# Hybrid attention and convolution layer: last six attention units spaced wider, second attention norm moved three steps back

## The chip, the cores and the metric

One core of one Trainium2 chip runs one program. The metric is the device time in microseconds (us) of an execution. Engines by the profile's names: PE is TensorE's matmul, PEld its weight load, DVE VectorE, ACT ScalarE, POOL GpSimd, SP SyncE. SBUF is the on-chip memory, PSUM the memory that PE writes. L642 is line 642 of the kernel.

## The reference, cut to what matters

```python
h = rms_norm(x, norm_mix_g)                    # x: (1, 1024, 1024) float32
q, k, v, u, gate = jnp.split(h @ w_in, splits, axis=-1)
q, k = rms_norm(q per head), rms_norm(k per head)
a = sliding_window_gqa(q, k, v, sinks, rel_bias)   # window 128, 8 heads of 64, 2 kv heads
c = conformer_conv(u, gate, ...)               # 512 channels
mix = jnp.concatenate([rms_norm(a, attn_out_g), rms_norm(c, conv_out_g)], axis=-1)
x = x + mix @ w_out
x = x + jnp.square(jax.nn.relu(rms_norm(x, norm_mlp_g) @ w_mlp_up)) @ w_mlp_down
```

Only the attention `a`, its norm, and where both stand among the matmuls of `mix @ w_out` are touched.

## The kernel before

All activations lie with features on the 128 partitions and tokens along the free side; the 1024 tokens are two halves h = 0 and 1 of 512. A dense product is made with each operand split in two parts (`whi`, `wlo` of the weight, the first and second slice of `mix` or `x1g` of the activation) and three matmuls of 128x128 by 128x512 for each block.

**Dense steps.** `build` (L212) runs a chain of generators, `dense`, one step at a time. Steps 0 to 47 are the input projections. Steps 48 to 55 are `out_conv(0)` and 56 to 63 `out_conv(1)` (L711): the half of the output projection that reads the convolution's `mix`, one step for each of 8 row blocks, 12 matmuls a step, and DVE adds the product to x (L720). Steps 64 to 71 are `out(0)` and 72 to 79 `out(1)` (L723): the other half, that reads the attention's `mix`, 12 matmuls a step, DVE adds again (L731). From step 80 `up_first` begins the MLP. Each step also has ACT and DVE split the weights of the next one (L162, L163).

**Side work.** Ahead of each dense step the words of `SIDE[k]` (L40) are issued. An attention unit is one of 4 head pairs j and one of 4 pairs of query blocks bp, named by the digits "j bp", and has three words:
- `A` (`attn_a` L551 and `attn_b` L576): score matmuls into two `sc` banks (`sc<-kh,Q`), four ACT copies to an SBUF tile `s` (L571), bias and maximum on DVE (L572), four Exp on ACT (L586), scaling on DVE (L592).
- `T` (`attn_t`): eight transposes of `s` into two `tr` banks (`tr<-ident,s`, L89) and two DVE copies to a tile `pT` (L596).
- `V` (`attn_v`): the products with v into the one `o` bank (`o<-pT,v`) and an ACT copy over the unit's slice of `Q` (L596).

The twelve late units, in the order of `U_LATE` (10, 11, 20, 21, 30, 31, 12, 13, 22, 23, 32, 33), have their `A` at the steps of `LATE`, `T` three steps and `V` five steps later. Units with bp 0 and 1 make half 0, bp 2 and 3 half 1.

**Norms.** `N0` and `N1` (`norm_attn`, `norm_half` L623) norm the attention of half 0 and 1 over four head pairs, each by three words: squares on ACT and sums on DVE (`nacc`, L628 to L632); a sum over partitions on PE into the `o` bank (`o<-ones,nacc`), DVE (L206) and a power on POOL (L207); a broadcast on PE into an `sc` bank (`sc<-ident,rc`), then for each of the four pairs a scaling on DVE (L642), an ACT cast (L652) and a DVE subtraction (L653), which make that half's `mix`. `out(0)` can't begin before N0's `mix`, `out(1)` not before N1's.

**Buffers and order.** PSUM has two banks each of `mm` (dense products), `sc` and `tr`, one of `o` and one of `x`. The tiles `s` and `pT` share eight SBUF buffers of tag `t`. The order on each engine is fixed when the program is built: from the program's order, from what is pinned, and from when inputs and buffers come free; so an instruction may stand on its engine before or behind the step that issued it. Units and norms issue no DMA.

Of the kernel before, what the change touches and what calls it, by code (L numbers as in the profile page):

```python
# [35 lines left out]
EVAC = {11: 'vaa', 2: 'aaa', 0: 'aaa', 9: 'vav', 10: 'avv', 8: 'vaa', 6: 'vav', 12: 'aaa', 4: 'aaa', 14: 'aav', 13: 'vaa', 3: 'aav', 15: 'aav', 1: 'aaa', 7: 'aaa', 5: 'aaa'}  # L36
ORDER = "u0,u1,u2,u3,v,q1,q2,q3"
U_EARLY, U_LATE = (9, 13, 17, 21), ("10", "11", "20", "21", "30", "31", "12", "13", "22", "23", "32", "33")
LATE = (43, 44, 47, 48, 51, 51, 52, 53, 54, 55, 56, 57)
SIDE = {2: "rs", 3: "st4 st0", 5: "rb st0", 6: "st4", 7: "st4", 12: "c0", 20: "c1", 28: "c2",  # L40
# [5 lines left out]
for n, at in enumerate(U_EARLY):  # L46
    SIDE[at] = SIDE.get(at, "") + f" A0{n}"
    SIDE[at + 4] = SIDE.get(at + 4, "") + f" T0{n}"
    SIDE[39 + n] = SIDE.get(39 + n, "") + f" V0{n}"
for u, at in zip(U_LATE, LATE):  # L50
    SIDE[at] = SIDE.get(at, "") + " A" + u
# [1099 lines left out]
```

## Time and profile before

| What | us |
|---|---|
| Median of 3 runs | 995.53 (990.51 to 996.84) |
| The profiled execution | 990.88 |
| Its span, first to last instruction | 989.1 |

The span is 1.78 us shorter than the profiled execution. PE's share is time in which a matmul is under way; matmuls overlap, so a busy PE can still be waiting inside one. Places in the trace are us from the start of the span. Counted by its matmuls, PE's steps 48 to 63 begin at 235.4, step 64 at 319.8, step 72 at about 345.8.

### The profile page before, as it was taken

How to read it: one execution, taken by the hardware profiler on the slowest of the kernel's cores; microseconds unless marked ns; L12 is line 12 of the kernel's file. 1: busy time of each engine (PE TensorE's matmuls, PEld its weight loads, DVE VectorE, ACT ScalarE, POOL GpSimd, SP SyncE). 2: the span in 40 equal slices, each digit the busy share in tenths (PEclk: the TensorE clock that was granted, in tenths of full speed). 3: DMA queues.
4: the chain of work that ended last, by engine and by line, in shares of the span. 5: the costliest groups of instructions: out<-in, count | busy, mean ns of one | idle time of the engine just before them, and what ended most of it. 6: DMA issues, size and time to landing. Idle time of an engine off the chain costs nothing.

```text
span 989.1 us, 14838 instructions
## 1 busy us (share of the span) xinstructions
PE 976.7 (99%) x5560; PEld 798.0 (81%) x5560; DVE 683.5 (69%) x1250; ACT 490.9 (50%) x938; POOL 29.3 (3%) x25
## 2 busy tenths in 40 slices
PE   8999999999999999999999999999999999999998
PEld 6887887878777777788888888888888888888886
DVE  6456554537888888976777777867775777647763
ACT  7436632396676456754444545545354344443442
POOL 1300000103000000000000000000000000000000
PEclk9999999997999999999999999999999999999999
DMA  9112232000431134464657566586975533336451
GB/s 353 52 63 92 81 107 64 12 12 21 141 106 65 64 116 150 175 230 149 235 201 242 180 217 220 198 285 194 328 253 190 179 103 103 109 128 232 152 170 43
DMA packets 67464, 148.71 MB, mean 150 GB/s; under 512 B 7777, under 2 KB 8033, under 8 KB 66881
## 3 DMA queue, kind: packets, MB, share of 16 engines
q1 hardware_dynamic: 67248, 147.75, 43.5%
q8 instruction: 44, 0.72, 0.3%
q14 instruction: 28, 0.22, 0.1%
q10 hardware_dynamic: 144, 0.02, 0.0%
HBM read 106.98 MB, written 38.80 MB: 147 GB/s over the span
## 4 chain that ended last, share of the span: by engine, by line
PE 91%; DVE 4%; ACT 2%; DMA 1%; issue 1%; SPq 0%; DVEq 0%; ACTq 0%
PE mm L86 37%; PE sc L86 26%; PE tr L86 17%; PE o L86 5%; PE x L86 4%; PE tr L89 1%; DMA xraw<-xT 1%; DVE Q L642 1%; DMA wd<-w_down 1%; ACT wb L756 0%; SPq L135 0%; DVE wlo L163 0%; DVE X L1068 0%; ACT y L693 0%; DVE wb L757 0%
## 5 line engine op out<-in xcount | busy, mean ns | idle before, releaser
L86 PE MATMUL sc<-op,wb 128*128 128x512 f32 x576 | 136.6, 389 | 0.0
L86 PEld LDWEIGHTS sc<-op,wb 128*128 128x128 f32 x576 | 108.1, 188 | 22.4
L756 ACT CAST wb<-wd 128x512 fp32r<-128x512 f32 x80 | 49.7, 622 | 111.3 <-DVE wd L1019 41.9
L757 DVE TENSOR_TENSOR wb<-wd,wb 128x512 fp32r<-128x512 f32 x80 | 55.3, 691 | 69.8 <-ACT wb L756 69.8
L86 PE MATMUL mm<-wb,wb 128*128 128x512 f32 x384 | 103.1, 389 | 0.1
L86 PE MATMUL sc<-wb,wb 128*128 128x512 f32 x384 | 102.9, 389 | 0.0
L86 PE MATMUL tr<-op,wb 128*128 128x512 f32 x384 | 91.3, 389 | 0.0
L86 PE MATMUL mm<-mix,whi 128*128 128x512 f32 x256 | 82.9, 401 | 1.8 <-DVE mix L653 0.8
L86 PEld LDWEIGHTS mm<-wb,wb 128*128 128x128 f32 x384 | 72.0, 188 | 15.4 <-ACT wb L756 0.5
L86 PEld LDWEIGHTS sc<-wb,wb 128*128 128x128 f32 x384 | 72.1, 188 | 15.0
L86 PEld LDWEIGHTS tr<-op,wb 128*128 128x128 f32 x384 | 72.1, 188 | 14.9
L86 PE MATMUL tr<-wb,wb 128*128 128x512 f32 x288 | 78.4, 389 | 0.1
L86 PE MATMUL mm<-xh,whi 128*128 128x512 f32 x192 | 77.7, 405 | 0.0
L86 PE MATMUL mm<-xh,wlo 128*128 128x512 f32 x192 | 77.0, 401 | 0.0
L757 DVE TENSOR_TENSOR wb<-hb,wb 128x512 fp32r<-128x512 f32 x112 | 76.7, 685 | 0.0
L86 PE MATMUL mm<-xl,whi 128*128 128x512 f32 x192 | 76.5, 398 | 0.0
L162 ACT CAST whi<-raw 128x512 fp32r<-128x512 f32 (+1 forms) x54 | 42.7, 794 | 66.7 <-PE mm L86 54.4
L756 ACT CAST wb<-hb 128x512 fp32r<-128x512 f32 x112 | 69.0, 616 | 0.3 <-PE sc L86 0.3
L756 ACT CAST wb<-raw 128x512 fp32r<-128x512 f32 x46 | 27.8, 622 | 74.7 <-PE tr L86 22.9
L86 PEld LDWEIGHTS tr<-wb,wb 128*128 128x128 f32 x288 | 54.0, 188 | 11.7 <-ACT wb L756 0.5
L163 DVE TENSOR_TENSOR wlo<-raw,whi 128x512 fp32r<-128x512 f32 (+1 forms) x54 | 48.6, 901 | 18.3 <-ACT whi L162 18.3
L86 PEld LDWEIGHTS mm<-mix,whi 128*128 128x128 f32 x256 | 46.6, 188 | 14.1 <-issue 3.4
(228 smaller groups left out, 1757.7 us busy)
## 6 DMA issues: line engine op xcount, KB each, us to landing
hb<-hid SPq DMA_DIRECT2D x112, 256.0 KB, 2.9
wd<-w_down SPq DMA_DIRECT2D x80, 256.0 KB, 4.2
raw<-w_up SPq DMA_DIRECT2D x27, 512.0 KB, 3.6
hid<-h SPq DMA_DIRECT2D x48, 256.0 KB, 2.9
pa<-pa SPq DMA_DIRECT2D x20, 512.0 KB, 4.6
raw<-w_out SPq DMA_DIRECT2D x32, 256.0 KB, 2.6
hid<-pa SPq DMA_DIRECT2D x32, 256.0 KB, 2.8
hid<-tu SPq DMA_DIRECT2D x32, 256.0 KB, 2.8
```

What stands on the lines that cost most here:

```text
L86: self.put(self.tc.nc.tensor.matmul(*a, **k))
L89: self.put(self.tc.nc.tensor.transpose(*a, **k))
L162: self.pin(nc.scalar.copy(hi, raw))
L163: self.pin(eng.tensor_tensor(lo, raw, hi.bitcast(F32), ALU.subtract))
L642: nc.vector.scalar_tensor_tensor(s, s, self.pv[:, goff + j:goff + j + 1], rb, ALU.mult, ALU.mult)
L756: self.pin(self.nc.scalar.copy(hi, src))
L757: self.pin(eng.tensor_tensor(lo, src, hi.bitcast(F32), ALU.subtract))
```

## The change

Two edits of tables. In `LATE`, the `A` steps of the last seven entries change: unit 31 from 51 to 52, 12 from 52 to 53, 13 from 53 to 55, 22 from 54 to 56, 23 from 55 to 58, 32 from 56 to 59, 33 from 57 to 61; their `T` and `V` move with them, so V33 goes from step 62 to 66. (30 stays at 51.) The three words of `N1` go from steps 65, 66, 67 to 68, 69, 70. `N0` stays at 59, 60, 61. No instruction is added or removed.

```diff
-LATE = (43, 44, 47, 48, 51, 51, 52, 53, 54, 55, 56, 57)
+LATE = (43, 44, 47, 48, 51, 52, 53, 55, 56, 58, 59, 61)
...
-        59: "N0", 60: "N0", 61: "N0", 65: "N1", 66: "N1", 67: "N1", 73: "X0", 74: "X0 G0", 75: "G0 G0", 76: "G0 G0", 77: "G0 G0",
+        59: "N0", 60: "N0", 61: "N0", 68: "N1", 69: "N1", 70: "N1", 73: "X0", 74: "X0 G0", 75: "G0 G0", 76: "G0 G0", 77: "G0 G0",
```

## Rows read from the trace of the kernel before

**Rows 1.** The page, span and busy time of each engine.
```profile
span 989.1 us, 14838 instructions
PE 976.7 (99%) x5560; PEld 798.0 (81%) x5560; DVE 683.5 (69%) x1250; ACT 490.9 (50%) x938; POOL 29.3 (3%) x25
```

**Rows 2.** Chain of waits, whole span: start us, us, what.
```profile
432.33 2.72 PE sc L86 x12
```

**Rows 3.** Busy time by stretch; the columns stand in its first line.
```profile
core 0: us, PE busy (x) PEld busy (x) DVE busy (x) ACT busy (x) POOL busy (x), PEclk, DMA share, GB/s
...
284.00:304.00 20.00, 20.00 (x128) 14.76 (x125) 17.47 (x67) 15.92 (x53) 0.00 (x0) 1.00 0.22 71
...
314.10:322.40 8.30, 6.92 (x76) 5.49 (x74) 7.16 (x14) 4.74 (x10) 1.01 (x1) 1.00 0.10 34
...
333.90:345.80 11.90, 11.75 (x56) 9.44 (x55) 11.72 (x19) 7.18 (x12) 0.00 (x0) 1.00 0.26 88
```

**Rows 4.** Timeline of PE, 311 to 324: start us, us, instruction [idle before <-releaser].
```profile
311.65 1.09 PE L86 MATMUL o<-pT,v 128*64 128x128 f32 x16
312.68 1.09 PE L89 MATMUL tr<-ident,s 128*128 128x128 f32 x8
313.53 0.48 PE L86 MATMUL mm<-mix,whi 128*128 128x512 f32 x1
...
314.08 0.95 PE L86 MATMUL o<-ones,nacc 128*128 128x1 f32 x8
314.88 1.07 PE L89 MATMUL tr<-ident,s 128*128 128x128 f32 x8
...
317.18 1.16 PE L86 MATMUL sc<-ident,rc 128*128 128x128 f32 x8
...
319.83 0.73 PE L86 MATMUL mm<-mix,whi 128*128 128x512 f32 x2 [0.47 <-DVE Q L642]
320.49 1.09 PE L86 MATMUL o<-pT,v 128*64 128x128 f32 x16
322.36 0.50 PE L86 MATMUL mm<-mix,whi 128*128 128x512 f32 x1 [0.77 <-DVE mix L653]
```

**Rows 5.** Timeline of DVE, lines of both attention norms.
```profile
295.11 0.68 DVE L632 TENSOR_TENSOR nacc<-nacc,sq 128x512 f32<-128x512 f32 x1
...
318.37 2.72 DVE L642 SCALAR_TENSOR_TENSOR Q<-Q,pv,sc 128x512 f32<-128x512 f32 x4 [1.14 <-PE sc L86]
...
324.03 0.68 DVE L632 TENSOR_TENSOR nacc<-nacc,sq 128x512 f32<-128x512 f32 x1
...
335.28 2.72 DVE L642 SCALAR_TENSOR_TENSOR Q<-Q,pv,sc 128x512 f32<-128x512 f32 x4
...
338.52 1.29 DVE L653 TENSOR_TENSOR mix<-Q,mix 128x512 fp32r<-128x512 f32 x2
...
340.92 1.29 DVE L653 TENSOR_TENSOR mix<-Q,mix 128x512 fp32r<-128x512 f32 x2
```

**Rows 6.** Timeline of PE, attention units and N1, other windows.
```profile
266.82 1.14 PE L86 MATMUL sc<-kh,Q 64*128 64x256 f32 x8
...
297.19 1.09 PE L86 MATMUL o<-pT,v 128*64 128x128 f32 x16
...
327.48 0.95 PE L86 MATMUL o<-ones,nacc 128*128 128x1 f32 x8
333.88 1.05 PE L86 MATMUL sc<-ident,rc 128*128 128x128 f32 x8
```

**Rows 7.** Busy time by stretch, dense matmuls (`mm`) alone: us, PE (x), clock, DMA.
```profile
235.30:266.80 31.50, 23.73 (x94) 1.00 0.32 105
```

**Rows 8.** Busy time by stretch, at and behind idle PE.
```profile
166.90:169.00 2.10, 0.35 (x24) 0.18 (x14) 0.00 (x0) 0.97 (x2) 0.00 (x0) 1.00 0.00 0
169.00:172.40 3.40, 3.40 (x96) 2.84 (x97) 0.58 (x1) 1.16 (x2) 0.00 (x0) 0.50 0.02 5
...
223.60:233.80 10.20, 10.14 (x50) 9.51 (x51) 5.24 (x14) 4.48 (x9) 5.68 (x3) 0.50 0.00 0
```

## Prediction

> **What bounds the kernel now.** I read the page's first part, then the chain, then the busy times by stretch, then PE's timeline where a stretch lacked something. PE is busy for 976.7 of 989.1 us and DVE for 683.5 [rows 1]: the kernel is bound by PE's stream of matmuls. The busy share alone hides small waits, so the pace is needed beside it: twelve matmuls of 512 columns take 2.72 us on the chain [rows 2], 0.227 each, and one step of the output projection is twelve. In the stretch that the change touches, PE has no idle time from 284 to 304 (20.00 of 20.00), while DVE is at 17.47 of 20; from 314.1 to 322.4 PE is busy for only 6.92 of 8.30 [rows 3]. That hole is the one place where `out(0)` waits. The reader is to see in it that the last dense matmul of `out_conv(1)` goes at 313.53 or right behind it, and that `out(0)` runs two matmuls at 319.83 and the rest from 322.36, released by DVE's Q and `mix`, the lines of N0 [rows 4].
>
> Why N0 is late: its sum is complete at 295.11 + 0.68 = 295.8 [rows 5], but its `o<-ones` goes at 314.08 [rows 4], 18.3 us later. There is one `o` bank, and the matmuls on it stand in program order: V31, V12, V13, V22 (one of them at 297.19 [rows 6], V22 at 311.65), then N0's sum, then V23, V32 and V33, the last at 320.49 [rows 4]. V13 (step 58) and V22 (59) are issued ahead of N0's second word (60). So N0 queues for a bank behind units of the other half.
>
> **The change part by part.** No work is added or taken away on any engine; all of it is order. All seven moved units keep what they issue: 8 score matmuls, 8 transposes and 16 value matmuls as the trace records them, 4 ACT copies out of `sc` and 4 Exps, and their DVE work. They issue no DMA and nothing on POOL, so SP's and POOL's queues are passed by nothing but N1's one power, which still follows N0's and precedes X0's.
>
> *N0's place in the queue: a gain.* With V13 at step 60 (behind N0's word, which stands first in that step), V22 at 61 and V23 at 63, the `o` order becomes V31, V12, N0's sum, V13. N0's sum can then go right behind V12: 297.19 + 1.09 = 298.3 at the earliest [rows 6] instead of 314.08. Its broadcast needs an `sc` bank, for which it now stands ahead of A33 instead of behind all units; 3.1 us lie between the two before (314.08 to 317.18), and 5.2 more until the first `mix` matmul of the full stream (322.36) [rows 4]: 298.3 + 8.3 = 306.6. DVE is at 87% in that stretch [rows 3], so I allow twice the last 5.2: 311.8, still ahead of 314. What the hole is worth: the work in it, at the distances between starts in [rows 4 and 6], is the sum 0.80, eight transposes 0.85, three V at 1.03, the broadcast 0.80 (333.88 to 334.68, where the next matmul starts) and two matmuls 0.45, together 6.0 of 8.28 us from 314.08 to 322.36. So 2.3 us of waiting goes. The lower bound of the gain is 0 (the wait moves), the upper one 2.3 and the few tenths of pieces like 312.68 to 313.53; I take 2.3, by the 18.3 us that the sum stood ready.
>
> *The units further apart: nothing.* From 284 to 304 PE has no idle time to give back [rows 3], so a unit's position there costs PE the same. What hides the units' ACT and DVE work is the dense stream. Eight buffers serve `s` and `pT`; in the new order A13 stands behind T31 and A22 behind T12, so units start later than now. If this cover is gone, it shows as a late V33 (rival 4). What is queued behind a unit on DVE are the steps' own additions and weight splits, and PE waits for those.
>
> *N1 three steps back: a loss.* PE reaches `out(1)` at 334.68 + 48 x 0.227 = 345.6, with the small gaps 345.8; less the gain, 343.5. Before, N1's sum goes at 327.48, behind 24 of the 96 matmuls of `out(0)`; its broadcast at 333.88, behind 48 [rows 6]. From the broadcast's start to the end of the first `mix` subtraction are 338.52 + 0.65 - 333.88 = 5.3 us, to the third 340.92 + 0.65 - 333.88 = 7.7 [rows 5, 6]; DVE is at 11.72 of 11.90 there [rows 3], so this doesn't shrink. Now the sum stands behind 60 matmuls, and at the same distance of 24 the broadcast stands behind 84. Then 12 matmuls are left, 2.72, and the broadcast itself 0.80: PE is at `out(1)` 3.5 us behind the broadcast's start, and the first `mix` comes at 5.3. Wait: 1.8. The third comes at 7.7, PE at 5.3 + 6 x 0.227 = 6.7: up to 1.0 more if DVE keeps its additions between them. If instead the broadcast follows the sum as closely as N0's did (3.1 us [rows 4]), `mix` is there before PE. Bounds: 0 and 2.8. I take 1.8, since the same norm's own distance is the nearest row. Behind N1's broadcast on DVE wait the steps' additions and splits, and PE waits for these; they stand inside the 5.3.
>
> Sum against the profiled execution: 990.9 - 2.3 + 1.8 = 990.4, a change of -0.5 us. That execution lies 4.6 us under the median of 995.53, whose three runs span 6.3. The forecast for the median is 995.0.
>
> **The rivals.**
> 1. *Nearly even* (the forecast): 995.0. Likeliest own range, from the bounds: 992.9 (all of the gain, no loss; a few tenths of pieces are within the rounding) to 998.3 (no gain, loss of 2.8).
> 2. *N1 stays hidden.* Its chain is short where PE isn't in between (3.1 us). Then 995.5 - 2.5 = 993.0. Against it: DVE is full around it.
> 3. *The change doesn't do what it says.* Units already run behind their place: A31, issued at step 51, goes at 266.82 [rows 6], after 94 of the dense matmuls that begin at 235.4 [rows 7], which is 7.8 steps of twelve behind step 48, so 4.8 late. If buffers set the starts, N0 may still meet a full DVE and the hole may stay or move: 995.5, or 997.3 with N1's 1.8.
> 4. *Slower: V33 is late, and N1 with it.* The place is the start of `out(1)`. Without a wait N1's sum would go 36 matmuls and 1.6 us before 343.5, at 333.7. Before, V33 started at 320.49, and N1's last addition ended at 324.03 + 0.68, 4.2 us later [rows 4, 5]. So it decides from a V33 later than 329.5, 9.0 us behind today's. Price: if V33 is 4.8 steps late, as A31 is, it goes at step 70.8, 1.2 steps or 3.3 us ahead of 343.5, at 340.2; then 340.2 + 4.2 + 3.1 + 5.3 = 352.8 for `mix`, against 345.8 today: +7.0. For it speaks the lag of A31 that rival 3 counts; against it, that the wider spacing gives each unit more of DVE. An idle stretch can also bring the lower clock: after 166.9 to 169.0, with PE busy for 0.35 of 2.10, the clock is 0.50 of full, that is 1.2 of 2.4 GHz, for 3.4 us [rows 8]; that adds 1.7. Together +8.7: 1004.2.
> 5. *Faster than the sum.* From 223.6 to 233.8 the clock is 0.50 [rows 8], a price of 10.2 / 2 = 5.1 us. If the new order reached back so far, 995.5 - 5.1 - 2.3 = 988.1. Against it: nothing issued before step 51 changes.
>
> The Trainium skill, in "TensorE: Matmul & The Clock Gate", section "HAM oscillation — how this bites in real kernels", says that PE left idle while it waits for operands loses its full clock and starts the next group slow. The trace agrees at 169.0 with its 0.50 [rows 8]. It doesn't agree that such a wait must do it: the hole at 314 kept its clock at 1.00 [rows 3]. By the rule a wait of N1 would add a slow stretch, 995.0 + 1.7 = 996.7; by the row of the hole it adds nothing. I follow the hole, which is the same kind of wait with work in between.
>
> **How the numbers follow.** Chances: forecast 0.47, hidden 0.22, no effect 0.15, late 0.12, far faster 0.04. The range: low 989.0, between rival 5 and rival 2; high 1002.0, most of the way to rival 4, since its price grows with each step that V33 is late. That leaves out about 2 in 10, and covers the scatter of the runs. A measurement tells about 1% from no change, here 10 us. More than that faster needs 985.5, below every case: 0.03. More than that slower needs 1005.5, the tail of rival 4: 0.05. Within: 0.92.
>
> **What would show it.** Right: N0's `o<-ones` two V's earlier, near 300; the stretch before `out(0)` without idle PE; N1's broadcast behind some 84 matmuls of `out(0)`, and 1 to 3 us of waiting for `mix` (L653) or Q (L642) at the start of `out(1)`. Wrong: the hole still there; V33 later than 329.5; PE's clock at 0.50 past 300; more or less idle PE from 358 on, where I changed nothing.

## The result, and the profile after

| | before | after |
|---|---|---|
| Median of 16 runs, us | 994.68 (990.51 to 997.75) | 1001.2 (996.84 to 1003.1) |
| Span of the profiled execution, us | 989.1 | 1001.0 |
| A31's first score matmul to the first MLP matmul, us | 103.89 | 110.16 |
| From there to the end of the span, us | 618.4 | 618.3 |

After over before is 1.0063, 95% interval 1.0047 to 1.0078. The change costs about 6.5 us where the forecast was a gain of 0.5; the median lies inside the range, the sign is wrong. Seven units move, 31 to 33 in `LATE`; the title's "last six" leaves out 31.

The two profiled executions differ by 11.9 us. Of this 5.7 lie ahead of A31 (272.51 against 266.82), where the two programs issue the same work: near 42 us the clock is at 0.50 for 10.2 us in after and 3.4 in before, which at half speed makes 3.4 of the 5.7. That is scatter between executions and not the change: in the four kernels below with the units and banks of before A31 goes at 269.53 to 272.72, in the four with those of after at 266.44 to 273.22. So everything below counts from A31's first score matmul. The change's 6.27 us all lie between it and the MLP, as the last two rows of the table show.

The page of after, span and busy time of each engine:

```profile
span 1001.0 us, 14845 instructions
PE 986.4 (99%) x5560; PEld 804.3 (80%) x5560; DVE 684.2 (68%) x1250; ACT 491.2 (49%) x938; POOL 28.7 (3%) x25
```

Beside [rows 1] nothing is to be seen: PE is 99% busy in both. The loss shows in the busy time by stretch. After, from the last units to the start of `out(1)` (us, PE busy, PEld, DVE, ACT, POOL, clock, DMA share, GB/s):

```profile
300.00:320.00 20.00, 20.00 (x144) 15.73 (x145) 17.20 (x57) 13.60 (x45) 1.12 (x1) 1.00 0.23 78
320.00:351.50 31.50, 31.21 (x180) 24.07 (x179) 24.44 (x53) 16.40 (x36) 1.50 (x1) 1.00 0.20 68
351.50:364.70 13.20, 10.21 (x35) 7.98 (x34) 6.64 (x13) 3.55 (x6) 1.01 (x1) 0.74 0.06 21
355.60:362.40 6.80, 6.80 (x21) 5.64 (x22) 2.27 (x5) 0.00 (x0) 1.01 (x1) 0.50 0.01 2
```

The hole of [rows 3], 1.38 us without PE, is gone ahead of `out(0)`. A new one of 3 us stands at the start of `out(1)`, and the clock is at 0.50, that is 1.2 of 2.4 GHz, for 6.8 us behind it. PE's timeline of after (start, us, instruction, idle time before it and what ended it):

```profile
272.51 1.14 PE L86 MATMUL sc<-kh,Q 64*128 64x256 f32 x8
...
306.69 0.72 PE L86 MATMUL o<-ones,nacc 128*128 128x1 f32 x6
...
315.53 1.16 PE L86 MATMUL sc<-ident,rc 128*128 128x128 f32 x8
...
331.05 1.23 PE L89 MATMUL tr<-ident,s 128*128 128x128 f32 x8
332.43 0.50 PE L86 MATMUL mm<-mix,wlo 128*128 128x512 f32 x1 [0.16 <-DVE wlo L163]
...
335.42 1.09 PE L86 MATMUL o<-pT,v 128*64 128x128 f32 x16
...
347.00 0.95 PE L86 MATMUL o<-ones,nacc 128*128 128x1 f32 x8
...
350.67 1.05 PE L86 MATMUL sc<-ident,rc 128*128 128x128 f32 x8
353.52 0.73 PE L86 MATMUL mm<-mix,whi 128*128 128x512 f32 x2 [1.80 <-ACT mix L652]
355.45 1.76 PE L86 MATMUL x<-ones,rbc 128*128 128x1 f32 x8 [1.19 <-DVE rbc L737]
357.07 0.77 PE L86 MATMUL mm<-mix,whi 128*128 128x512 f32 x1
...
364.70 1.05 PE L86 MATMUL x<-ident,rc 128*128 128x128 f32 x8
...
382.67 0.61 PE L86 MATMUL mm<-x1g,whi 128*128 128x512 f32 x2
```

This answers to [rows 4 and 6]. N1's sum went behind 24 of `out(0)`'s 96 matmuls, now behind 84; its broadcast behind 48, now behind all 96. The broadcast takes 0.81 of PE, so PE is at `out(1)` at 351.48, 78.97 behind A31 (before 346.16 - 266.82 = 79.34). From there to the MLP it takes 31.19 instead of 24.55. The parts of these 6.64 us: 353.52 - 351.48 = 2.04 of waiting for the first `mix`; then 3.55 for two matmuls (0.45) and X0's sum (0.81), 2.29 lost; then 7.63 for 22 matmuls worth 4.99, 2.64 lost to the clock. That makes 6.97, 0.3 more than the difference. Of the 2.29, 1.19 are idle time and 0.81 are the clock too, since X0's sum runs slow (355.45 to 357.07, 1.62 instead of 0.81). So the clock costs 2.64 + 0.81 = 3.45, about half of the 6.64. X0's sum, the squares of `out(0)` summed over partitions, waits there for the last addition of L737, which DVE makes behind four scalings of N1. The chain of waits of after (start, us, what) says the same:

```profile
347.95 2.90 PE mm L86 x12
...
351.48 0.68 DVE wlo L163
352.16 2.63 DVE Q L642 x4
354.79 0.61 DVE rbc L737
...
355.45 1.76 PE x L86 x8
357.21 7.65 PE mm L86 x22
```

Why N1's sum is so late is on ACT. Its timeline after, squares of `out(0)` (L736) and of N1 (L628, L631):

```profile
335.79 0.63 ACT L736 ACTIVATE sq<-Xp 128x512 f32<-128x512 f32 x1 [0.34 <-DVE Xp L731]
339.76 0.63 ACT L736 ACTIVATE sq<-Xp 128x512 f32<-128x512 f32 x1 [0.28 <-DVE Xp L731]
340.30 0.61 ACT L628 ACTIVATE nacc<-Q 128x512 f32<-128x512 f32 x1
340.82 1.14 ACT L631 ACTIVATE sq<-Q 128x512 f32<-128x512 f32 x2
342.37 0.63 ACT L631 ACTIVATE sq<-Q 128x512 f32<-128x512 f32 x1
```

and before:

```profile
293.87 0.61 ACT L628 ACTIVATE nacc<-Q 128x512 f32<-128x512 f32 x1
306.36 0.63 ACT L631 ACTIVATE sq<-Q 128x512 f32<-128x512 f32 x1
317.64 0.63 ACT L631 ACTIVATE sq<-Q 128x512 f32<-128x512 f32 x1
322.05 0.63 ACT L631 ACTIVATE sq<-Q 128x512 f32<-128x512 f32 x1
```

Before, each square ran as its head pair came ready, the first one 26 us ahead of `out(0)`. After, all four go right behind the square of `out(0)`'s step 67. Both kinds take their tile by `half` (L128), from the tag `sq` with three buffers; N1's `nacc` does too, since `sq` is the tag that `half` gives by default, so N1 asks for four tiles. In program order N1's word at step 65 takes them ahead of `out(0)`'s squares of steps 65 to 67, at step 68 behind these. Theory: this tag holds N1 back, not the step of its sum. Rivals: V33, which goes 62.9 us behind A31 instead of 53.7; and the steps of N1's other words.

### The profile page after: what moved, and what is told of

Its sections match the earlier page's. It is cut to its first block, busy times and chain, and to the rows that moved or that the text cites. A ratio compares the mean times of both kernels' runs of the same rounds, so it can differ in the third digit from the quotient of the medians.

```text
span 1001.0 us, 14845 instructions
## 1 busy us (share of the span) xinstructions
PE 986.4 (99%) x5560; PEld 804.3 (80%) x5560; DVE 684.2 (68%) x1250; ACT 491.2 (49%) x938; POOL 28.7 (3%) x25
## 4 chain that ended last, share of the span: by engine, by line
PE 91%; DVE 4%; ACT 2%; issue 1%; DMA 1%; SPq 0%; DVEq 0%; ACTq 0%
PE mm L86 37%; PE sc L86 26%; PE tr L86 17%; PE o L86 6%; PE x L86 4%; PE tr L89 1%; DVE X L1068 0%; ACT wb L756 0%; DMA hid<-pa 0%; DMA xraw<-xT 0%; SPq L135 0%; DVE wb L757 0%; ACT y L693 0%; ACT s L586 0%; DVE wlo L163 0%
## 5 line engine op out<-in xcount | busy, mean ns | idle before, releaser
L86 PE MATMUL tr<-op,wb 128*128 128x512 f32 x384 | 91.3, 389 | 0.0
L86 PE MATMUL mm<-mix,whi 128*128 128x512 f32 x256 | 85.2, 411 | 1.8 <-ACT mix L652 1.8
L163 DVE TENSOR_TENSOR wlo<-raw,whi 128x512 fp32r<-128x512 f32 (+1 forms) x54 | 48.6, 902 | 20.6 <-ACT whi L162 20.6
```

The source lines that it names most:

```text
L86: self.put(self.tc.nc.tensor.matmul(*a, **k))
L163: self.pin(eng.tensor_tensor(lo, raw, hi.bitcast(F32), ALU.subtract))
```

## The experiments

Times are beside the median of before on the same chip; "a/b" is the number of `out(0)`'s 96 matmuls ahead of N1's sum and broadcast (before 24/48, after 84/96); the stretch is A31 to the MLP.

**N1 alone.** Before, with the N1 edit and not the units'.

```diff
-65: "N1", 66: "N1", 67: "N1",
+68: "N1", 69: "N1", 70: "N1",
```

> The kernel before with only N1 moved to steps 68, 69, 70; the units stay where they were. Measure beside the whole time: from A31's scores to the first matmul of the MLP, 103.9 us in the trace of before, 110.2 in that of the changed kernel. Theory S (N1's squares share three buffers with the squares of out(0), so that moving N1's first word behind those of out(0) makes its squares wait for them, whatever the units do): the squares run some 17 us later than the values are ready, N1's sum stands behind 84 of the 96 matmuls of out(0), its broadcast behind all 96, and PE waits at out(1) as in the changed kernel; the hole before out(0) also stays, so 110 to 113 in the stretch, whole time 6 to 9 us over before. Rival U (the late units make V33 late, and N1 with it): V33 is as early as before, so N1 follows its steps, behind 60 and 84 matmuls, and the stretch is 104 to 106, the whole time 0 to 2 us over before.

84/96; stretch 110.09; 1001.41 against 995.16, ratio 1.0054 (1.0031 to 1.0078). PE's timeline:

```profile
270.84 1.14 PE L86 MATMUL sc<-kh,Q 64*128 64x256 f32 x8
...
324.40 1.09 PE L86 MATMUL o<-pT,v 128*64 128x128 f32 x16
...
348.99 1.05 PE L86 MATMUL sc<-ident,rc 128*128 128x128 f32 x8
351.85 0.73 PE L86 MATMUL mm<-mix,whi 128*128 128x512 f32 x2 [1.80 <-ACT mix L652]
353.77 1.86 PE L86 MATMUL x<-ones,rbc 128*128 128x1 f32 x8 [1.19 <-DVE rbc L737]
```

V33 goes at 324.40, 53.6 behind A31 as before, and still the same two waits stand at `out(1)`, followed by 6.8 us of clock at 0.50. N1's move makes the whole loss; V33 isn't needed for it.

**Own tiles for N1's squares.** After, with `nacc` and the squares, all four, in two tiles of tag `t`. The same edit on the N1-alone kernel is the next one.

```diff
-        acc = self.half("nacc")
+        own = kc0 == 0 and h == 1
+        ts = [self.tmp("nq", (P, 2, HT)) for _ in range(2)] if own else None
+        acc = ts[0][:, 0] if own else self.half("nacc")
...
-                sq = self.half("sq")
+                sq = ts[j // 2][:, j % 2] if own else self.half("sq")
```

> The changed kernel, with N1's squares and sum in two buffers of their own (tag t, free by then) instead of the three shared with out(0). Theory S: the squares run as soon as the values are there, N1's sum stands behind about 60 matmuls of out(0) and its broadcast behind 84, the wait at out(1) is 0 to 2 us instead of 7 with its slow clock, the stretch from A31 to the MLP 103 to 105, the whole time within 2 us of before. Rival U: V33 is as late as in the changed kernel, the sum stays late, the stretch stays at 109 to 111 and the whole time 5 to 7 us over before.

60/84; stretch 105.32; 996.78 against 995.16, ratio 1.0013 (0.9992 to 1.0035). The one wait left at `out(1)` stands at its third matmul, and the clock stays at 1.00:

```profile
341.18 0.95 PE L86 MATMUL o<-ones,nq 128*128 128x1 f32 x8
347.57 1.05 PE L86 MATMUL sc<-ident,rc 128*128 128x128 f32 x8
352.95 0.50 PE L86 MATMUL mm<-mix,whi 128*128 128x512 f32 x1 [1.35 <-DVE mix L655]
```

**N1 alone, own tiles.**

> The kernel before with N1 at steps 68, 69, 70 as in the first of these runs, and its squares in two buffers of their own. Theory S: the program step itself is not what makes N1 late, so N1 runs as early as before, sum behind 24 and broadcast behind 48 matmuls, and the stretch is 103.5 to 104.5, the whole time as before within 1.5 us. Rival P (an instruction can't go ahead of its program step, which I held in the prediction): sum behind 60, broadcast behind 84, stretch 105 to 107.

24/48; stretch 103.82; 994.78 against 995.16, ratio 1.0006 (0.9987 to 1.0025). N1's words stand at 68 to 70, and its sum (331.54) and broadcast (337.97) go exactly as far into `out(0)` as in before:

```profile
331.54 0.95 PE L86 MATMUL o<-ones,nq 128*128 128x1 f32 x8
337.97 1.05 PE L86 MATMUL sc<-ident,rc 128*128 128x128 f32 x8
```

So the steps of the words cost nothing; the shared tag of the first one's tiles costs everything. The last two kernels differ only in the units' edit: with it V33 is late, N1's sum goes behind 60 instead of 24, and the stretch is 1.50 longer.

**The squares one step earlier**, after with N1 at 67, 69, 70; and **the later words earlier**, after with all three words at 68 (one run).

```diff
-68: "N1", 69: "N1", 70: "N1",
+67: "N1", 69: "N1", 70: "N1",
```

> The changed kernel with only N1's first word (its squares) one step earlier, 67 instead of 68, so that it stands ahead of the square of out(0)'s step 67; its two later words stay at 69 and 70. The stretch from A31's scores to the MLP is 103.9 us in before, 110.2 in the changed kernel, 105.3 with buffers of its own. Theory S (the place of the squares in the queue for the shared buffers sets N1): the sum comes a step or two earlier, some matmuls of out(0) stand between broadcast and out(1), the stretch is 104.5 to 107.5, the clock keeps full speed at out(1), whole time 0.5 to 3.5 us over before. Rival P (the places of the later words set it): 109.5 to 110.5, 6 us over before.

```diff
-68: "N1", 69: "N1", 70: "N1",
+68: "N1 N1 N1",
```

> The counterpart: the changed kernel with N1's second and third word earlier, all three at step 68, the squares where they were. Theory S: nothing changes, sum behind 84 and broadcast behind 96 matmuls of out(0), stretch 109.5 to 110.7. Rival P: one to two steps come back, stretch 104 to 108.

With the squares at 67: 62/84, stretch 105.30, 996.37 against 995.0, ratio 1.0009 (0.9984 to 1.0033). ACT's timeline has N1's squares right behind the square of step 66:

```profile
336.46 0.63 ACT L736 ACTIVATE sq<-Xp 128x512 f32<-128x512 f32 x1 [0.33 <-DVE Xp L731]
337.00 0.61 ACT L628 ACTIVATE nacc<-Q 128x512 f32<-128x512 f32 x1
```

With the later words at 68: 84/96, stretch 110.11, the same two waits, 1002.57 in its one run. One step of the first word is worth 4.9 us of the stretch, two steps of the third nothing.

**N1 one step later, in before** (one run).

```diff
-65: "N1", 66: "N1", 67: "N1",
+66: "N1", 67: "N1", 68: "N1",
```

> The kernel before with N1 one step later, at 66, 67, 68, units unchanged: a small dose of the move. Theory S: each step puts another square of out(0) ahead of N1's in the shared buffers; one step costs N1 two steps (sum behind about 50 matmuls, broadcast behind 72), but PE still has 24 matmuls left, 5.4 us and 0.8, against the 5.3 that the first mix needs: no wait, stretch 103.5 to 104.5. If the loss grew evenly with the move (rival: 6.2 us over three steps), it would be 106.

50/72; stretch 104.07 (+0.18); 998.77 in its one run, whose excess lies outside the stretch. On ACT N1's squares go right behind that of step 65:

```profile
333.82 0.61 ACT L736 ACTIVATE sq<-Xp 128x512 f32<-128x512 f32 x1
334.34 0.62 ACT L628 ACTIVATE nacc<-Q 128x512 f32<-128x512 f32 x1
```

The loss is no steady price for each step: it begins when the cover of `out(0)`'s remaining matmuls is used up.

**X0's sum held behind `out(1)`'s first step**, in after.

```diff
+        with self.tc.issue_after(self.pe.last) if h == 0 else ExitStack():
```

(around the four sum matmuls of `x1_norm`; `pe.last` is the matmul issued last.)

> The changed kernel, with X0's sum over partitions held behind the first step of out(1) on PE, instead of behind its first two matmuls. It tells what part of the 7 us at out(1) belongs to X0's sum standing ahead of the dense matmuls and waiting for the last square sum of out(0). Theory S with its parts: the 1.8 us wait for mix stays, the 1.2 us wait of X0's sum goes; whether the clock still falls to 0.50 is open. If it does, the stretch shortens by 1 to 2 us; if it doesn't, by 3 to 5. Rival C (X0's sum alone made the loss, N1 would have been in time): the stretch falls to 104.

84/96; stretch 108.72, 1.44 less than after; 1000.11 against 995.16, ratio 1.0052 (1.0032 to 1.0072). The second wait isn't X0's alone: with X0 out of the way, PE waits for the second slice of `mix` (L653), and the clock is at 0.50 for 3.4 us instead of 6.8.

```profile
347.42 0.73 PE L86 MATMUL mm<-mix,whi 128*128 128x512 f32 x2 [1.80 <-ACT mix L652]
349.94 0.79 PE L86 MATMUL mm<-mix,whi 128*128 128x512 f32 x1 [1.79 <-DVE mix L653]
```

**N0 earlier instead of units later**, before with N0 at 57 to 59: the hole closed by another way.

```diff
-        59: "N0", 60: "N0", 61: "N0",
+        57: "N0", 58: "N0", 59: "N0",
```

> The kernel before with N0 alone two steps earlier, at 57, 58, 59; units and N1 stay. It takes away the hole ahead of out(0) without the rest of the change. My prediction's first term (the hole is worth 2.3 us): stretch 101.5 to 102, whole time 2 us under before. Rival M (the waiting only moves: the units behind N0 are late by N0's work on DVE, the last of them hold up N1, and PE waits at out(1) instead): no hole at out(0), N1's sum behind about 72 matmuls and its broadcast behind 96, stretch 106 to 110, whole time 2 to 6 us over before.

The hole is gone, and PE is at `out(1)` 77.58 behind A31, 1.8 earlier than before. But unit 33 stands behind N0's work on DVE (its scaling, L592, goes at 322.99, behind N0's last L653), and V33 goes at 333.31, 63.8 behind A31. N1, unmoved, is at 72/96 and meets the same two waits of 1.80 and 1.19, with 3.4 us of slow clock. Stretch 107.16; 999.05 against 995.0, ratio 1.0045 (1.0022 to 1.0067). So a late V33 can make N1 late by itself, as rival 4 had it; in after N1's squares go even later than V33 makes them.

**One unit a step, own tiles for N1.** The units at 51 to 58.

```diff
-LATE = (43, 44, 47, 48, 51, 51, 52, 53, 54, 55, 56, 57)
+LATE = (43, 44, 47, 48, 51, 52, 53, 54, 55, 56, 57, 58)
```

> A version between the two: the last seven units one step later than before (31 at 52 to 33 at 58), N0 and N1 at the places of before, N1's squares in two buffers of their own. If a small shift of V13 and V22 lets N0's sum go ahead without delaying V33, part of the hole's 2.3 us comes back: stretch 102.5 to 103.7, whole time 0 to 1.5 us under before. Otherwise it stays at 103.9.

24/48; stretch 106.65; 998.2 against 995.0, ratio 1.0051 (1.0025 to 1.0076). N1 is in time, but `out(0)` begins 54.70 behind A31 (before 53.01) and PE is at `out(1)` at 82.11, 2.8 later, which is the whole loss; the forecast had 103.9 at most. The hole isn't wider: PE's idle time from N0's sum to the full stream of `out(0)` is 0.74 here and 1.38 before, though N0's sum still goes behind V13. What the units cost PE has changed. From A31 on, the distances from each of the 56 score matmuls to PE's next start add up to 12.93 instead of 10.64, which is 2.29 of the 2.77. Unit 22, before and here:

```profile
283.67 1.14 PE L86 MATMUL sc<-kh,Q 64*128 64x256 f32 x8
...
287.56 1.13 PE L86 MATMUL sc<-kh,Q 64*128 64x256 f32 x4
...
289.28 1.13 PE L86 MATMUL sc<-kh,Q 64*128 64x256 f32 x4
```

Eight in one go start in pairs, the two of a pair 0.01 apart, and take 1.06 of PE; in two groups of four they don't pair and take 2.12. Before, three of the seven units go in groups, here five. PE counts as busy in both forms.

**Norm broadcasts in the `x` bank**, three kernels: the table's `nb` alone; with N0 at 57 to 59; and with the sums (`ns`) there too.

```diff
-TAGS = {'qs': 'tr', 'kb': 'sc', 'vt': 'o', 'ns': 'o', 'nb': 'sc', 'ln': 'x', 'si': 'tr', 'x1': 'x'}
+TAGS = {'qs': 'tr', 'kb': 'sc', 'vt': 'o', 'ns': 'o', 'nb': 'x', 'ln': 'x', 'si': 'tr', 'x1': 'x'}
```

> The kernel before with one edit: the broadcast of both norms uses the x bank, idle in this stretch, instead of an sc bank behind the units' scores. Theory Q (the hole is made by the queue of the norms for banks that the units hold): N0's broadcast goes ahead of the end of out_conv(1), the hole goes, N1 stays in time, stretch 101.5 to 103, whole time 1 to 2.5 us under before. Rival M (the waiting only moves, as with N0 two steps earlier): 103.9 or more.

> The same with N0 at 57, 58, 59 as well. With N0 early alone the stretch was 107.2, because the units waited for N0's broadcast to free its sc bank and V33 came late. Theory Q: with the x bank the units go on, no hole and N1 in time: stretch 101.5 to 103, whole time 1 to 2.5 us under before. Rival M (N0's work on DVE delays the units in any case): 105 to 108.

> The same with N0's and N1's sums over partitions in the x bank too, so that neither queues behind a V in the o bank. Theory Q: as the one before or some tenths better, 101.3 to 103. Rival M: 105 to 108. If the conv norms, which use the same bank now, come later, it shows ahead of A31 and not in the stretch.

Against 995.3: 998.6, ratio 1.0033 (1.0014 to 1.0052); 995.52, ratio 1.0002 (0.9984 to 1.0021); 997.88, ratio 1.0029 (1.0012 to 1.0046). `nb` also serves the convolution's norms, so A31 moves and the stretch must be taken from `out_conv`'s first matmul to the MLP: 131.63, 130.39 and 132.08, before 135.33. The second one has the closed hole and N1 in time. It takes 24.29 from `out(0)` to `out(1)`, before 26.33, but 1.03 of these 2.04 are V33's matmuls, which stand ahead of `out(0)` there. And ahead of `out_conv`, from the 400th matmul of the input projection on, the three take 91.3, 87.1 and 87.6 instead of 81.3; 20 of the units' score matmuls have moved there, so a part of both differences is moved work. Together the two stretches take 223.0, 217.5 and 219.6, before 216.6: nothing is gained. No kernel here is faster than before.

## Why the prediction was wrong

**What bounds the kernel, the hole and its worth: right.** The hole's 2.3 us measured 1.8 in the kernel that closed it by moving N0 alone; no other run measures it by itself.

**N0's place in the queue: right in the order, not in the gain.** N0's sum goes two V's earlier, behind V12, and no PE is idle ahead of `out(0)`. It goes 34.2 us behind A31, which in the trace of before would be 301.0 and so near the 300 named, in two pieces with a unit's scores between; its broadcast goes 43.0 behind A31, before 50.4. But PE is at `out(1)` only 0.4 earlier than before; the N1-alone kernel, with the hole open, is there at 78.96. So the hole's gain was given back on the way. About 1 us of it is to be seen at 330 to 332.4: two `mix` matmuls (0.45) and eight transposes (0.85) take 2.25 from 330.18. DVE has the unit's scaling of `s` (L592) and the weight's split (L163) in one queue, and PE's next dense matmul waits for the split. By kind, from A31 to `out(1)`, PE's distances from start to start add up to 0.94 less at the V matmuls, where the hole's waits stood, and 0.43 less at the scores, but to 1.15 more at the transposes, which go in smaller groups.

**The units further apart, "nothing": right only beside this N1.** From the N1-alone kernel to after the stretch changes by 0.07. With N1 freed it costs 1.5, by way of V33. The reason given, that a unit's position costs PE the same where PE is never idle, is wrong: by position a unit's scores take 1.06 or 2.12, as the one-unit-a-step kernel shows. That the parts nearly cancel in after is luck.

**N1 three steps back: this step failed.** I put N1's sum behind 60 matmuls by the steps of its words and took the chain from the sum on. The steps hold nothing back: with own tiles and the units of before, the same words run at 24/48. What I left out is the first word, the squares. Only rival 4 has them, by what they read (V33); what they write is four tiles of a tag that `out(0)` uses in every step from 65 on. The measured place is 84/96, and the price at `out(1)` 6.64 instead of 1.8: 2.04 for the first `mix`, 2.29 at X0's sum, 2.64 at the matmuls behind it, less 0.3; 3.45 of it are the clock, a term that I put at nothing. The chain behind the broadcast was right: with X0 held back, PE goes on with the first L653's `mix` 5.38 behind the broadcast's start, forecast 5.3. In the kernels that put N1 at 60/84 and 62/84 (own tiles; squares at 67) the stretch is 1.43 and 1.41 longer than before, near the 1.8. But in the own-tiles kernel N1 stands there by way of V33 and not of its steps, so that this place was met is luck.

That the tag holds the squares is shown by own tiles, not how it does so in full. The first buffer, of step 65's square, was read for the last time at 332.29 (L737), and N1's squares still go behind the square of step 67. So in the trace it is no wait for a free buffer. In the kernels with N1's first word at 66, 67 and 68, `nacc`, the first of its four tiles, is written right behind the square of step 65, 66 and 67: this is what handing out the tiles of a tag in program order gives. The order on ACT is fixed when the program is built; that this is its rule, and which of the four tiles would have to be freed, no run shows.

**Rival 4 had the place and the size, not the cause.** It named the start of `out(1)`, 7.0 us of waiting and 1.7 for a slow clock; V33 even came 9.2 later, just past the 9.0 from which it was to decide. But N1 alone, with V33 in its old place, has the same loss. That the sizes are near is luck too: of the 6.64, only about half is waiting.

**The clock.** I followed the hole of [rows 3], which kept 1.00. The waits at `out(1)` of after did not: 1.80 and 1.19 us of idle time with two matmuls between, then 0.50 for 6.8 us, which cost 3.45 of the 6.64. The rule of the Trainium skill that I had set aside ("TensorE: Matmul & The Clock Gate", section "HAM oscillation — how this bites in real kernels"), that a wait for operands starts the next group slow, is borne out by this stretch and not by the 1.35 us wait of the own-tiles kernel. The waits in that section's example are longer than these; what such short ones do is told by these runs alone.

## What to carry to other kernels

When a step of a program is moved, list every buffer tag that its instructions take, also the one that a helper gives by default, and not only the banks and the inputs: a tag shared with the dense steps can hold the moved step behind them. Then say where the instructions come to stand by how many of the dense matmuls lie ahead, since the step number alone moved nothing here. A chain hidden behind such matmuls costs little until the cover is used up (50/72: 0.18 of stretch), and past that point its waits, here with the slower clock on top (84/96: 6.2). And a PE that is never idle can still take longer for the same matmuls: look at the distances between starts, and at whether they stand in one group.

## What was not expected of the hardware

The same two waits, 1.80 and 1.19 us, were followed by 6.8 us at 0.50 in three kernels (after, N1 alone, the later words earlier) and by 3.4 us in N0 earlier; 1.80 and 1.79 also by 3.4. A single one of 1.35 left the clock at 1.00. So what a wait of 1 to 2 us, or two of them, cost in clock was 0, or by estimate half of the slow stretch, 1.7 or 3.4 us; in after the matmuls of that stretch took 3.45 longer.
